# Feed-forward products by quarters with seven block products in place of eight

## The chip, the cores and the metric
The kernel runs on one core of a Trainium2 chip. Its engines are TensorE (PE, matmul), VectorE (DVE), ScalarE (ACT), GpSimd (POOL) and SyncE (SP, which issues the DMAs). The metric is the device time in microseconds: 1560.2 us is the median of three runs of the kernel before (1560.07 to 1561.64).

## The reference, cut to what matters
One layer of a hybrid encoder over 1024 tokens of 1024 channels: a norm and modulation, three token-mixing branches, a gated merge, an output projection with a residual, and a feed-forward of 4096 features with a squared ReLU.
```python
y = merged @ w_out
x = x + gate_m[:, None] * rmsnorm(y, g_mix_post)
h2 = rmsnorm(x, g_ff_pre) * (1.0 + scale_f[:, None]) + shift_f[:, None]
y2 = jnp.square(jax.nn.relu(h2 @ w_ff1)) @ w_ff2
return x + gate_f[:, None] * rmsnorm(y2, g_ff_post)
```
All is float32. The matrices of the two feed-forward products are 1024x1024 by 1024x4096, and 1024x4096 by 4096x1024.

## The kernel before
Every large product is made of two-part operands: a float32 tile a is split in hi (rounded to the fp32r format by ACT, line 99) and lo = a - hi (DVE, line 100), and each product takes three matmuls of 128x128 by 128x512: hi*hi, hi*lo, lo*hi. DVE's subtraction reads two SBUF operands.

The output projection (`out_tile`, L719 to L721) goes over eight token tiles of 128. The weights w_out come as eight raw tiles `wor` (L690), two in the buffers "raw" and six in the buffers "B", and are split to `woh` and `wol`. Behind each token tile stands a chain: squares of y on ACT (L722), a root with a Heron step (L212 to L219), the scaling by DVE (L729), the residual (L731), the store to x_d (L732), the second norm (L733, L735). `h2T_pair(tp, ...)` transposes two finished token tiles on PE (L744) and splits the result for the feed-forward (L752 to L755). The last pair's call stands inside the feed-forward: `ff1(0, ..., 0)`, then `h2T_pair(3, ...)`, then three more `ff1`.

The feed-forward goes over chunks of two feature tiles (the last of four). Per feature tile f, `ff1` makes u = relu(h2 @ w1)^2 for two halves of 512 tokens with 24 matmuls each (gemm_T, L327 to L329); ACT takes the ReLU from PSUM (L774), DVE squares (L775), and u is split. Then the chunk's u is multiplied with its two rows of w_ff2 for eight token tiles and two halves of the features (L820 to L822), and DVE adds the sum into `yacc` in SBUF (L827; one operand in PSUM). u never leaves SBUF. Per product of the feed-forward that is 8*32*2*3 = 1536 matmuls. POOL does nothing here until the end, where it multiplies by the gate row (L831). The last chunk's token tiles carry the final norm and the stores.

The instructions of each engine run in the order in which a scheduler puts them at build time. A tile whose tag has `bufs` buffers waits for the last reader of the tile that held its buffer before; one pool `big` holds all tiles for the whole program.

Of the kernel before, what the change touches and what calls it, by code (L numbers as in the profile page):

```python
# [51 lines left out]
def kernel(  # L52
# [389 lines left out]
    def att_scores(hd, cq, QS, KH, KL, nck):  # L442
        # softmax rows of queries 256 cq .. 256 cq + 255
# [43 lines left out]
    def att_values(hd, cq, Pt, att):  # L487
# [34 lines left out]
    def pool_unit(m):  # L522
# [4 lines left out]
        # trailing sums over 2, 4, 8, 16 tokens by doubling  # L527
# [103 lines left out]
    def mod_rows():  # L631
# [3 lines left out]
        # rows of gate * post-norm gain  # L635
# [36 lines left out]
        # the branches one after another for the last tile, which frees their operands earlier  # L672
# [28 lines left out]
    h2T = [None] * KT  # L701

    def out_tile(t):
        # x + gate * norm(merged @ w_out) for 128 tokens; the normalised result stays in xt
        tk = slice(t * P, (t + 1) * P)
        xt = sb("raw" if (t // 2) % 2 == 0 else "G", name="x2")
        nc.sync.dma_start(xt, x[t])
        mh = sb("whi", F32R, (P, KT, P), name="mh")
        ml = sb("wlo", F32R, (P, KT, P), name="ml")
# [4 lines left out]
        yt = sb("G", name="yt")  # L714
# [192 lines left out]
```

## Time and profile before
| | us |
|---|---|
| median of three runs | 1560.2 |
| span of the profiled execution | 1558.6 |
| PE busy | 1531.4 (98%) |
| DVE busy | 844.7 (54%) |
| ACT busy | 480.4 (31%) |
| POOL busy | 154.0 (10%) |

The profiled execution's span begins with its first instruction and ends with its last; the runs' times lie 1.5 us and more above it. A matmul's own duration is pipelined, so that the price of one in a row is the distance of two starts. "PE clock" in the rows is the granted clock as a share of the full one. The rows on which the prediction rests stand in a section of their own below.

### The profile page before, as it was taken

To read this page: it belongs to the slowest core of one execution; us is meant where nothing else is said; L and a number is where in the kernel's file an instruction comes from. 1 tells how busy PE (TensorE), PEld (TensorE's weight loads), DVE (VectorE), ACT (ScalarE), POOL (GpSimd) and SP (SyncE) were. 2 spreads that over 40 slices of the span, in tenths; PEclk is the share of its full clock that TensorE was granted. 3 is DMA by queue.
4 is the path that set the end of the run, shared out by engine and by line. 5 is a ranking of instruction groups with operands and counts; after the bars stand their busy time and mean duration, and the time that the engine had idled before them with its cause. 6 is when DMAs were issued, how large, how long until landed. Compare 5 with 4: busy or idle time off the path is not lost.

```text
span 1558.6 us, 18251 instructions
## 1 busy us (share of the span) xinstructions
PE 1531.4 (98%) x7115; PEld 1248.2 (80%) x7115; DVE 844.7 (54%) x1746; ACT 480.4 (31%) x876; POOL 154.0 (10%) x203
## 2 busy tenths in 40 slices
PE   6999999999999999999999999999999999999997
PEld 4897777777788888888888888888888888888886
DVE  7643578786685443222677344444444554444447
ACT  4612344445631111111555522221111222221132
POOL 6301323233300000000000000000000000000013
PEclk9999999999999999999999999999999999999999
DMA  7511101202344433111424111111111111111124
GB/s 255 195 41 55 41 28 55 82 28 77 126 162 146 152 123 94 46 49 55 149 81 148 56 55 54 54 41 41 41 44 52 54 55 54 54 41 48 46 82 162
DMA packets 37376, 125.63 MB, mean 81 GB/s; under 512 B 4825, under 2 KB 5929, under 8 KB 37290
## 3 DMA queue, kind: packets, MB, share of 16 engines
q1 hardware_dynamic: 37290, 124.47, 24.4%
q8 instruction: 56, 0.92, 0.3%
q14 instruction: 30, 0.25, 0.0%
HBM read 112.35 MB, written 12.10 MB: 80 GB/s over the span
## 4 chain that ended last, share of the span: by engine, by line
PE 93%; DVE 3%; ACT 2%; DMA 1%; issue 0%; SPq 0%; DVEq 0%; ACTq 0%
PE ps_mm L327 16%; PE ps_mm L329 16%; PE ps_mm L328 16%; PE ps_s L822 5%; PE ps_s L820 5%; PE ps_s L821 5%; PE ps_av L510 3%; PE ps_s L468 2%; PE ps_av L820 2%; PE ps_av L822 2%; PE ps_av L821 2%; PE ps_s L467 1%; PE ps_s L329 1%; PE ps_s L327 1%; PE ps_s L328 1%; PE ps_pt L504 1%
## 5 line engine op out<-in xcount | busy, mean ns | idle before, releaser
L327 PE MATMUL ps_mm<-hT,whi 128*128 128x512 f32 x592 | 235.0, 397 | 0.0
L329 PE MATMUL ps_mm<-hT,wlo 128*128 128x512 f32 x592 | 233.6, 395 | 0.0
L328 PE MATMUL ps_mm<-hT,whi 128*128 128x512 f32 x592 | 233.2, 394 | 0.0
L329 PE MATMUL ps_mm<-h2h,wlo 128*128 128x512 f32 x512 | 199.4, 389 | 0.0
L327 PE MATMUL ps_mm<-h2h,whi 128*128 128x512 f32 x512 | 199.4, 389 | 0.0
L328 PE MATMUL ps_mm<-h2l,whi 128*128 128x512 f32 x512 | 199.4, 389 | 0.0
L100 DVE TENSOR_TENSOR wlo<-wr,whi 128x1024 fp32r<-128x1024 f32 x60 | 73.5, 1224 | 179.6 <-ACT whi L99 179.4
L774 ACT ACTIVATE fr<-ps_mm 128x512 f32<-128x512 f32 x64 | 38.2, 597 | 419.9 <-PE ps_mm L329 419.9
L827 DVE TENSOR_TENSOR yacc<-yacc,ps_s 128x512 f32<-128x512 f32 (+1 forms) x155 | 105.4, 684 | 69.0 <-PE ps_s L822 68.7
L775 DVE TENSOR_TENSOR fr<-fr 128x512 f32<-128x512 f32 x64 | 44.3, 692 | 174.7 <-ACT fr L774 174.7
L821 PE MATMUL ps_s<-w2l,uh 128*128 128x512 f32 (+1 forms) x356 | 137.6, 387 | 0.0
L820 PE MATMUL ps_s<-w2h,uh 128*128 128x512 f32 (+1 forms) x356 | 137.6, 387 | 0.0
L822 PE MATMUL ps_s<-w2h,ul 128*128 128x512 f32 (+1 forms) x356 | 137.6, 387 | 0.0
L327 PEld LDWEIGHTS ps_mm<-hT,whi 128*128 128x128 f32 x592 | 111.2, 188 | 25.8 <-issue 3.8
L329 PEld LDWEIGHTS ps_mm<-hT,wlo 128*128 128x128 f32 x592 | 111.2, 188 | 24.1 <-issue 2.6
L328 PEld LDWEIGHTS ps_mm<-hT,whi 128*128 128x128 f32 x592 | 111.2, 188 | 23.9 <-issue 2.4
L831 POOL TENSOR_TENSOR yl<-yacc,gfb 128x512 f32<-128x512 f32 (+1 forms) x16 | 20.1, 1273 | 1070.2 <-DVE yacc L827 1066.9
L99 ACT ACTIVATE whi<-wr 128x1024 fp32r<-128x1024 f32 x60 | 63.7, 1061 | 172.2 <-PE ps_mm L328 88.5
L328 PEld LDWEIGHTS ps_mm<-h2l,whi 128*128 128x128 f32 x512 | 96.1, 188 | 19.9
L327 PEld LDWEIGHTS ps_mm<-h2h,whi 128*128 128x128 f32 x512 | 96.2, 188 | 19.9
L329 PEld LDWEIGHTS ps_mm<-h2h,wlo 128*128 128x128 f32 x512 | 96.1, 188 | 19.9
L821 PEld LDWEIGHTS ps_s<-w2l,uh 128*128 128x128 f32 x356 | 66.9, 188 | 13.6
(297 smaller groups left out, 2705.7 us busy)
## 6 DMA issues: line engine op xcount, KB each, us to landing
wa<-in_w_ada_dram SPq DMA_DIRECT2D x48, 512.0 KB, 5.3
wr<-in_w_in_dram SPq DMA_DIRECT2D x40, 512.0 KB, 3.6
wr<-in_w_ff_dram SPq DMA_DIRECT2D x32, 512.0 KB, 3.6
w2r<-in_w_ff_dram SPq DMA_DIRECT2D x32, 512.0 KB, 3.5
x<-in_x_dram SPq DMA_DIRECT2D x16, 512.0 KB, 3.7
nck<-nck_d SPq DMA_DIRECT2D x8, 512.0 KB, 3.7
wr<-in_w_branch_dram SPq DMA_DIRECT2D x8, 512.0 KB, 3.6
wor<-in_w_out_dram SPq DMA_DIRECT2D x8, 512.0 KB, 5.9
```

The lines of the kernel that those rows point to most:

```text
L99: A.activation(hi, src, AF.Copy)
L100: V.tensor_tensor(out=lo, in0=src, in1=f32(hi), op=ALU.subtract)
L327: T.matmul(p, a, r0, start=(i == 0), stop=False)
L328: T.matmul(p, a, r1, start=False, stop=False)
L329: T.matmul(p, b, r0, start=False, stop=(i == n - 1))
L510: last_pe[0] = T.matmul(av[:, :256], st, PT[:, pp, offs[jj]:offs[jj] + 256], start=(j == 0 and pp == 0), stop=(j == nj - 1 and pp == 1))
L774: A.activation(r, p, AF.Relu)
L775: V.tensor_tensor(out=r, in0=r, in1=r, op=ALU.mult)
L820: T.matmul(p, us[i][0][:, tk], w2[i][0][:, ns], start=(i == 0), stop=False)
L821: T.matmul(p, us[i][0][:, tk], w2[i][1][:, ns], start=False, stop=False)
L822: T.matmul(p, us[i][1][:, tk], w2[i][0][:, ns], start=False, stop=(i == n_f - 1))
L827: V.tensor_tensor(out=ya, in0=ya, in1=p, op=ALU.add)
```

## The change
Both feed-forward products are cut in 2x2 quarters, and each takes seven block products in place of eight, with sums of blocks on both sides (the variant of Strassen's scheme with the fewest sums).

- **First product.** With h2 in quarters B11, B12, B21, B22 (channels by tokens) and w_ff1 in pairs of tiles j and 16+j, each of the 16 steps j makes seven products of 12 matmuls: `first_two` two (banks X and Y), `last_five` five. 16*7*12 = 1344 matmuls. The sums on the weights' side are four POOL additions of 128x512 for each j (`prep_s`); the sums T1 to T4 on h2's side are made once, after `first_two` of j = 0 to 3 (EARLY), by 4*4 DVE and 4*4 POOL additions of 128x512, each sum split by ACT and DVE. u is squared by one DVE instruction (L854), and its quarters are written to the DRAM buffer u_d, four stores of 256 KB for each j.
- **Second product.** u is read back in quarters uA, uB, uC, uD, 32 loads of 512 KB (quarters 0, 1 and 3 stay in SBUF, 8 buffers each; uC has 2), and w_ff2, laid out by quarters, is read in 512 KB blocks. Seven rounds of eight steps of 24 matmuls: 7*8*24 = 1344. Every step has a split of u and one of w (two ACT, two DVE instructions of 128x1024); the sums of blocks are 48 POOL additions of 128x1024 and 16 on DVE (lines 999 and 1013). uh, ul, wh, wl and the raw tiles `w2r` have two buffers each. The rounds are called here, in their order: X (into p1), Y, Z, X2, X3, Z2, X5.
- **Order.** `h2T_pair(3, ...)` now stands before the first matmul of the feed-forward. The raw tiles of w_out share four buffers with the tiles of x. The pools are opened and closed by stage, and a tile of a later stage waits for those tiles of an earlier one whose place it takes.
- **End.** The final norm runs over the token tiles after the last product; the half that comes last is scaled on DVE for the lower four tiles.

The core of the diff:
```diff
+    wpool = open_pool("wpool", side="right")
+    h2pool = open_pool("h2pool")
+    opool = open_pool("opool")
...
     for k in range(KT):
-        raw = sb("raw" if k < 2 else "B", name="wor")
+        raw = tile_of(opool, "x2", 4, name="wor")
         nc.sync.dma_start(raw, w_out[k])
...
+    B11, B21, B22 = ([tile_of(h2pool, "h2", 12, HT, F32R, name=n) for _ in range(4)] for n in ("b11", "b21", "b22"))
+    B12 = [tile_of(h2pool, "b12", 4, (P, HALF)) for _ in range(4)]
...
+                b = B11[k] if k < 4 else (B22 if tp >= 2 else B21)[k - 4]
                 h = small.tile([P, 256], F32, tag="t256", name="h2t", bufs=2)
-                A.activation(h, p[:, kk * 256:(kk + 1) * 256], AF.Identity,
-                             bias=modc[:, 24 + k:25 + k], scale=af[:, k:k + 1])
-                V.tensor_copy(hi, h)
-                V.tensor_tensor(out=lo, in0=h, in1=f32(hi), op=ALU.subtract)
+                A.activation(h, src, AF.Identity, bias=modc[:, 24 + k:25 + k], scale=af[:, k:k + 1])
...
+    h2T_pair(3, pairs[3])
...
+    def prep_a(j):
+        r = load_half(j)
+        o = tile_of(fpool, "op", 4, (P, 2, D), F32R)
+        fsplit(o[:, 0, :], o[:, 1, :], r)
+        return r, o
+    def prep_s(j, r1):
+        r2 = load_half(NJ + j)
+        K1, K2 = slice(0, HALF), slice(HALF, D)
+        s21, s34 = (tile_of(mpool, "M", 8, name=n) for n in ("s21", "s34"))
+        G.tensor_tensor(out=s21[:, K2], in0=r2[:, K1], in1=r2[:, K2], op=ALU.add)
+        G.tensor_tensor(out=s21[:, K1], in0=s21[:, K2], in1=r1[:, K1], op=ALU.subtract)
+        o21 = tile_of(fpool, "op", 4, (P, 2, D), F32R)
+        fsplit(o21[:, 0, :], o21[:, 1, :], s21)
+        G.tensor_tensor(out=s34[:, K1], in0=r1[:, K1], in1=r2[:, K1], op=ALU.subtract)
+        G.tensor_tensor(out=s34[:, K2], in0=r1[:, K2], in1=s21[:, K1], op=ALU.subtract)
+        o34 = tile_of(fpool, "op", 4, (P, 2, D), F32R)
+        fsplit(o34[:, 0, :], o34[:, 1, :], s34)
+        o4 = tile_of(fpool, "oc", 1, HT, F32R)
+        fsplit(o4[:, 0, :], o4[:, 1, :], r2[:, K2])
+        return o21, o34, o4
+    def product(p, o, c0, bs, start):
+        for k in range(4):
+            ks = slice(c0 + k * P, c0 + (k + 1) * P)
+            a, b = o[:, 0, ks], o[:, 1, ks]
+            r0, r1 = bs[k][:, 0, :], bs[k][:, 1, :]
+            T.matmul(p, a, r0, start=(start and k == 0), stop=False, skip_group_check=True)
...
+    def relu2(q, j, c):
+        r = tile_of(fpool, "ur", 3, (P, HALF))
+        V.scalar_tensor_tensor(out=r, in0=c, scalar=0.0, in1=c, op0=ALU.max, op1=ALU.mult)
+        nc.sync.dma_start(u_d[q, j // 2, :, j % 2, :], r)
...
+    def first_two(j):
+        r1, o = prep_a(j)
+        X = fbank("X", 5)
+        product(X, o, 0, B11, True)
+        s1 = snap(X)
+        Y = fbank("Y", 1)
+        product(Y, o, HALF, B21, True)
+        relu2(0, j, plus(Y, s1))
+        return X, r1
+    def last_five(j, X, r1):
+        o21, o34, o4 = prep_s(j, r1)
+        product(X, o21, 0, T2, False)
+        u2 = snap(X)
+        Z = fbank("Z", 2)
+        product(Z, o21, HALF, T1, True)
+        p5 = snap(Z)
+        product(X, o34, 0, T3, False)
+        relu2(3, j, plus(X, p5))
+        product(Z, o34, HALF, B22, False)
+        relu2(2, j, plus(Z, u2))
+        product(X, o4, 0, T4, False)
+        c = tile_of(fpool, "sn", 3, (P, HALF))
+        A.activation(c, X, AF.Relu)
+        relu2(1, j, c)
+    begun = [first_two(j) for j in range(EARLY)]
+    T1, T2, T3, T4 = ([tile_of(tpool, "t", 16, HT, F32R, name=n) for _ in range(4)] for n in ("t1", "t2", "t3", "t4"))
...
+    for k in range(4):
...
+        tsum(V, ta, B12[k], h11, ALU.subtract)
+        tsum(V, ta, ta, l11, ALU.subtract)
+        fsplit(T1[k][:, 0, :], T1[k][:, 1, :], ta)
+        tsum(V, ta, h22, ta, ALU.subtract)
+        tsum(V, ta, ta, l22, ALU.add)
+        fsplit(T2[k][:, 0, :], T2[k][:, 1, :], ta)
+        tsum(G, tb, ta, h11, ALU.subtract)
+        tsum(G, tb, tb, l11, ALU.subtract)
+        fsplit(T3[k][:, 0, :], T3[k][:, 1, :], tb)
+        tc_ = tile_of(fpool, "ur", 3, (P, HALF), name="tt")
+        tsum(G, tc_, h21, ta, ALU.subtract)
+        tsum(G, tc_, tc_, l21, ALU.add)
+        fsplit(T4[k][:, 0, :], T4[k][:, 1, :], tc_)
...
+            last_five(j, *first_two(j))
...
+    def step(bank, kk, uop, wop, ts=range(4), first=False, last=False):
+        for k in range(2):
+            for t in ts:
+                tk = slice(t * P, (t + 1) * P)
+                a, b = uop[0][:, k, tk], uop[1][:, k, tk]
+                r0, r1 = wop[0][:, k, :], wop[1][:, k, :]
+                T.matmul(bank[t], a, r0, start=(first and k == 0), stop=False, skip_group_check=True)
...
+    def parts(u, w):
+        uh, ul = g2("uh", 2, F32R), g2("ul", 2, F32R)
+        fsplit(uh, ul, u)
+        wh, wl = g2("wh", 2, F32R), g2("wl", 2, F32R)
+        fsplit(wh, wl, w)
+        return (uh, ul), (wh, wl)
...
+    uA = [load_u(0, kk, "uA", NK) for kk in range(NK)]
+    X = banks("X")
+    for kk in range(NK):
+        step(X, kk, *parts(uA[kk], load_b(0, kk)), first=kk == 0, last=kk == NK - 1)
+    p1 = copies(X)
+    uB = []
+    Y = banks("Y")
+    for kk in range(NK):
+        uB.append(load_u(1, kk, "uB", NK))
+        step(Y, kk, *parts(uB[kk], load_b(2, kk)), first=kk == 0, last=kk == NK - 1)
+    c11 = sums(Y, p1)
+    uD, tt = [], []
+    Z = banks("Y")
+    for kk in range(NK):
+        s1 = load_u(2, kk, "uC", 2)
+        uD.append(load_u(3, kk, "uD", NK))
+        G.tensor_tensor(out=s1, in0=s1, in1=uD[kk], op=ALU.add)
+        t1 = load_b(1, kk, "tt", NK)
+        b11 = load_b(0, kk)
+        V.tensor_tensor(out=t1, in0=t1, in1=b11, op=ALU.subtract)
+        tt.append(t1)
+        step(Z, kk, *parts(s1, t1), first=kk == 0, last=kk == NK - 1)
+        G.tensor_tensor(out=uA[kk], in0=s1, in1=uA[kk], op=ALU.subtract)
+    p5 = copies(Z)
+    for kk in range(NK):
+        b22 = load_b(3, kk)
+        G.tensor_tensor(out=tt[kk], in0=b22, in1=tt[kk], op=ALU.subtract)
+        step(X, kk, *parts(uA[kk], tt[kk]), last=kk == NK - 1)
+    u2 = copies(X)
+    for kk in range(NK):
+        b11 = load_b(0, kk)
+        V.tensor_tensor(out=b11, in0=tt[kk], in1=b11, op=ALU.subtract)
+        s3 = g2("uC", 2, name="u")
+        G.tensor_tensor(out=s3, in0=uD[kk], in1=uA[kk], op=ALU.subtract)
+        step(X, kk, *parts(s3, b11), last=kk == NK - 1)
+    c22 = sums(X, p5)
+    for kk in range(NK):
+        b22 = load_b(3, kk)
+        G.tensor_tensor(out=uB[kk], in0=uB[kk], in1=uA[kk], op=ALU.subtract)
+        step(Z, kk, *parts(uB[kk], b22), last=kk == NK - 1)
+    c12 = sums(Z, u2)
+    ops = []
+    for kk in range(NK):
+        b21 = load_b(2, kk)
+        G.tensor_tensor(out=b21, in0=b21, in1=tt[kk], op=ALU.subtract)
+        ops.append(parts(uD[kk], b21))
+        if kk < NK - 2:
+            step(X, kk, *ops[kk])
...
+            E = V if t >= 4 and n == 0 else G
...
-    def ff1(f, wts, u, hf):
-        cs = slice(hf * HALF, (hf + 1) * HALF)
-        p = gemm_T(wts, h2T, K8, hf, "mm")
-        r = sb("G", name="fr", shape=(P, HALF))
-        A.activation(r, p, AF.Relu)
-        V.tensor_tensor(out=r, in0=r, in1=r, op=ALU.mult)
-        split(u[0][:, cs], u[1][:, cs], r)
...
-            ff1(0, w1[0], us[0], 0)
-            h2T_pair(3, pairs[3])
-            ff1(1, w1[1], us[1], 0)
...
-            for n, (a, b) in enumerate(((0, 512), (512, 768), (768, 1024)) if tail else ((0, 512), (512, 1024))):
...
-                    V.tensor_tensor(out=ya, in0=ya, in1=p, op=ALU.add)
...
+        "w_ff2": a["w_ff2"][0].reshape(2, 8, 2, P, 2, HALF).transpose(0, 4, 1, 3, 2, 5).reshape(4, 8, P, 2, HALF),
```

PE at the end of the output projection. Before: `ff1` of feature tile 0 (ps_mm_7343) is issued, then the transposes of the last pair (x_964 is its first token tile, read by L744) stand between it and the matmuls of feature tile 1.
```order
L328 MATMUL ps_mm_7343<-h2l_6723,whi_7329 128x512
L329 MATMUL ps_mm_7343<-h2h_6722,wlo_7330 128x512
L327 MATMUL ps_mm_7343<-h2h_6728,whi_7329 128x512
L328 MATMUL ps_mm_7343<-h2l_6729,whi_7329 128x512
L329 MATMUL ps_mm_7343<-h2h_6728,wlo_7330 128x512
L744 MATMUL ps_pt_7373<-ident,x_964_7077 128x128
L744 MATMUL ps_pu_7386<-ident,x_964_7077 128x128
L327 MATMUL ps_mm_7425<-h2h_6671,whi_7335 128x512
L328 MATMUL ps_mm_7425<-h2l_6672,whi_7335 128x512
L329 MATMUL ps_mm_7425<-h2h_6671,wlo_7336 128x512
```
Now the same place in the changed kernel, with L776 for the transposes (x_974 is the pair's second token tile) and X for the first block product, which reads the split weights op and the quarter B11 (b_904):
```order
L776 MATMUL ps_pt_7343<-ident,x_964_7095 128x128
L776 MATMUL ps_pt_7343<-ident,x_974_7232 128x128
L776 MATMUL ps_pu_7356<-ident,x_964_7095 128x128
L776 MATMUL ps_pu_7356<-ident,x_974_7232 128x128
L776 MATMUL ps_pu_7356<-ident,x_964_7095 128x128
L776 MATMUL ps_pu_7356<-ident,x_974_7232 128x128
L847 MATMUL X_7386<-b_904_6393,op_7383 128x512
L848 MATMUL X_7386<-b_904_6393,op_7383 128x512
L849 MATMUL X_7386<-b_904_6393,op_7383 128x512
L847 MATMUL X_7386<-b_905_6394,op_7383 128x512
```
All transposes of the last pair have moved ahead of the first feed-forward matmul.

ACT in the feed-forward. Before, a pattern of three repeats from feature tile to feature tile (fr is u before the split):
```order
L774 ACTIVATE fr_8524<-ps_mm_8499 128x512
L99 ACTIVATE uh_8497<-fr_8524 128x512
L99 ACTIVATE w2h_8561<-w2r_8559 128x1024
L774 ACTIVATE fr_8554<-ps_mm_8529 128x512
L99 ACTIVATE uh_8497<-fr_8554 128x512
L99 ACTIVATE whi_8769<-wr_8767 128x1024
L774 ACTIVATE fr_8598<-ps_mm_8573 128x512
```
Now, around the sums T1 to T4 (sn_7510 is the copy of X in step j = 3, op_7722 and op_7727 the split weight sums of j = 1, t_... the splits of T1 to T4, sn_7650 the first copy of `last_five`; rows for k = 1 to 3 of the sixteen splits are the same as those of k = 0):
```order
L812 ACTIVATE op_7722<-s_1050_7718 128x1024
L859 ACTIVATE sn_7510<-X_7497 128x512
L812 ACTIVATE op_7727<-s_1051_7719 128x1024
L812 ACTIVATE t_1008_7529<-tt_7545 128x512
L812 ACTIVATE t_1012_7533<-tt_7545 128x512
L812 ACTIVATE t_1016_7537<-tt_7546 128x512
L812 ACTIVATE t_1020_7541<-tt_7559 128x512
L812 ACTIVATE t_1019_7540<-tt_7603 128x512
L812 ACTIVATE t_1023_7544<-tt_7616 128x512
L859 ACTIVATE sn_7650<-X_7386 128x512
L859 ACTIVATE sn_7665<-Z_7652 128x512
```
The splits of T1 to T4 stand behind the split of a weight sum for j = 1 and ahead of the first copy of `last_five`.

POOL in the feed-forward. Before, it has only the products with the gate row at the end:
```order
L831 TENSOR_TENSOR yl_11549<-yacc_7527,gfb_7323 128x512 x2
L831 TENSOR_TENSOR yl_11598<-yacc_7544,gfb_7323 128x512 x2
L831 TENSOR_TENSOR yl_11647<-yacc_7561,gfb_7323 128x512 x2
L831 TENSOR_TENSOR yl_11696<-yacc_7578,gfb_7323 128x512 x2
L831 TENSOR_TENSOR yl_11745<-yacc_7595,gfb_7323 128x512 x2
```
Now, from the third sum s1 of the round Z on (u_10282: L996 makes s1, L1002 the X operand of the next round, L1021 an operand of Z2, L1007 the weight sums of X2; 20 rows from the first of these to s1 of the last step, u_10497):
```order
L1021 TENSOR_TENSOR u_9972<-u_9972,u_9600 128x1024
L996 TENSOR_TENSOR u_10325<-u_10325,u_10327 128x1024
L1002 TENSOR_TENSOR u_9602<-u_10325,u_9602 128x1024
L1021 TENSOR_TENSOR u_10008<-u_10008,u_9602 128x1024
L996 TENSOR_TENSOR u_10368<-u_10368,u_10370 128x1024
L1002 TENSOR_TENSOR u_9604<-u_10368,u_9604 128x1024
L1021 TENSOR_TENSOR u_10044<-u_10044,u_9604 128x1024
L996 TENSOR_TENSOR u_10411<-u_10411,u_10413 128x1024
L1002 TENSOR_TENSOR u_9606<-u_10411,u_9606 128x1024
L1021 TENSOR_TENSOR u_10080<-u_10080,u_9606 128x1024
L1007 TENSOR_TENSOR w2r_10201<-w2r_10548,w2r_10201 128x1024
L1007 TENSOR_TENSOR w2r_10244<-w2r_10583,w2r_10244 128x1024
```
Three additions of 128x1024 stand on POOL for each step of Z from the third on. Behind s1 of Z's last step stand six more up to the seventh weight sum of X2 (L1007 of w2r_10459), and DVE's queue has, ahead of the splits of X2's first step, the first subtraction of X3 (L1013, w2r_10836), whose load takes a raw buffer that this seventh weight sum reads.

## Rows read from the trace of the kernel before
**Rows 1.** Page: busy time of the engines (1), and the chain by engine (4).
```profile
PE 1531.4 (98%) x7115; PEld 1248.2 (80%) x7115; DVE 844.7 (54%) x1746; ACT 480.4 (31%) x876; POOL 154.0 (10%) x203
PE 93%; DVE 3%; ACT 2%; DMA 1%; issue 0%; SPq 0%; DVEq 0%; ACTq 0%
```
**Rows 2.** Windows: start:end, length, busy (count) by engine, PE clock, DMA share, GB/s.
```profile
900.00:1000.00 100.00, 99.97 (x442) 82.48 (x441) 47.60 (x62) 22.59 (x31) 0.00 (x0) 1.00 0.16 48
...
1554.00:1556.00 2.00, 0.00 (x0) 0.00 (x0) 1.57 (x3) 0.00 (x0) 0.00 (x0) 0.56 0.06 24
```
**Rows 3.** Timeline at the output projection's start: start, length, engine, line, out<-in.
```profile
725.59 11.16 SPq L690 DMA_DIRECT2D wor<-in_w_out_dram  x2
...
750.53 1.06 ACT L99 ACTIVATE woh<-wor 128x1024 fp32r<-128x1024 f32 x1 [3.58 <-DMA wor<-in_w_out_dram]
751.81 1.06 ACT L99 ACTIVATE woh<-wor 128x1024 fp32r<-128x1024 f32 x1 [0.22 <-DMA wor<-in_w_out_dram]
...
755.64 0.39 PE L329 MATMUL ps_s<-brh,wlo 128*128 128x512 f32 x1
755.86 0.39 PE L719 MATMUL ps_mm<-woh,mh 128*128 128x512 f32 x1
```
**Rows 4.** Timeline and chain around the last pair of token tiles.
```profile
849.24 0.39 PE L327 MATMUL ps_mm<-h2h,whi 128*128 128x512 f32 x1
...
849.18 0.24 PE ps_s L721
...
853.97 4.42 DMA x_d<-x
...
858.42 0.77 DVE x L735
...
859.23 0.56 PE ps_pt L744 x3
...
862.54 0.66 PE ps_pu L744 x4
863.20 0.23 PE ps_mm L327
```
**Rows 5.** Groups by line and form: count, busy us, mean ns, idle before.
```profile
L100 DVE TENSOR_TENSOR ul<-fr,uh 128x512 fp32r<-128x512 f32 x64 | 44.4, 693 | 35.3 <-ACT uh L99 34.9
L100 DVE TENSOR_TENSOR w2l<-w2r,w2h 128x1024 fp32r<-128x1024 f32 x32 | 39.1, 1225 | 7.7 <-ACT w2h L99 7.7
...
L831 POOL TENSOR_TENSOR yl<-yacc,gfb 128x512 f32<-128x512 f32 x15 | 19.1, 1293 | 1070.2 <-DVE yacc L827 1066.9 <-issue 3.2
...
L107 POOL TENSOR_SCALAR whi<-wr 128x1024 fp32r<-128x1024 f32 x17 | 18.7, 1101 | 136.3 <-PE ps_mm L328 97.4 <-PE ps_s L328 26.4 <-issue 8.2
...
L99 ACT ACTIVATE w2h<-w2r 128x1024 fp32r<-128x1024 f32 x32 | 33.3, 1044 | 0.0
```
**Rows 6.** Timeline of POOL and DVE, where both run.
```profile
29.02 2.38 POOL L114 TENSOR_TENSOR wlo<-wr,whi 128x1024 fp32r<-128x1024 f32 x1 [3.72 <-ACT whi L113]
...
29.49 2.45 DVE L260 TENSOR_TENSOR hT<-h,hT 128x512 fp32r<-128x512 f32 x1 [1.17 <-ACT hT L259]
...
40.37 2.38 POOL L114 TENSOR_TENSOR wlo<-wr,whi 128x1024 fp32r<-128x1024 f32 x1 [1.91 <-ACT whi L113]
...
40.84 2.45 DVE L260 TENSOR_TENSOR hT<-h,hT 128x512 fp32r<-128x512 f32 x1 [2.37 <-ACT hT L259]
```
**Rows 7.** Timeline of PE near the program's start.
```profile
22.39 0.63 PE L327 MATMUL ps_av<-hT,whi 128*128 128x512 f32 x1
22.82 0.63 PE L328 MATMUL ps_av<-hT,whi 128*128 128x512 f32 x1
```
**Rows 8.** DMA issues: KB each, median us from issue to landing.
```profile
w2r<-in_w_ff_dram SPq DMA_DIRECT2D x32, 512.0 KB, 3.5
...
out_dram<-yl SPq DMA_DIRECT2D x16, 256.0 KB, 2.0
```
**Rows 9.** Timeline of PE, its last matmul.
```profile
1549.24 0.28 PE L822 MATMUL ps_s<-w2h,ul 128*128 128x256 f32 x1
```

More of the change, by code (lines that the diff above doesn't have):

```diff
@@ L762, with fbank, fsplit @@
         pairs.append((x0, out_tile(2 * tp + 1)))
-    yacc = [None] * NT
-    gfb = sb("G", name="gfb")
+    h2T_pair(3, pairs[3])
+    close_pool("opool")
+    close_pool("wpool")
+    close_pool("psum")
+    fpool = open_pool("fpool")
+    tpool = open_pool("tpool", side="right")
+    fps = open_pool("fps", space=bass.MemoryType.PSUM)
+    def fbank(tag, bufs):
+        return tile_of(fps, tag, bufs, (P, HALF))
+    def fsplit(hi, lo, src):
+        A.activation(hi, src, AF.Copy)
+        V.tensor_tensor(out=lo, in0=src, in1=f32(hi), op=ALU.subtract)
@@ new lines, in snap, with plus @@
+    def snap(p):
+        s_ = tile_of(fpool, "sn", 3, (P, HALF))
+        A.activation(s_, p, AF.Copy)
+        return s_
+    def plus(p, s_):
+        V.tensor_tensor(out=s_, in0=p, in1=s_, op=ALU.add)
+        return s_
+    def first_two(j):
[22 more added lines that the diff above has]
+        relu2(1, j, c)
@@ new lines, with g2, load_u @@
+    for j in range(NJ):
+        if j < EARLY:
+            last_five(j, *begun[j])
+        else:
+            last_five(j, *first_two(j))
+    for n in ("fpool", "h2pool", "mpool", "tpool", "fps"):
+        close_pool(n)
+    gpool = open_pool("gpool")
+    gps = open_pool("gps", space=bass.MemoryType.PSUM)
+    NK = NJ // 2
+    UT = (P, 2, HALF)
+    def g2(tag, bufs, dtype=F32, shape=UT, name=None):
+        return tile_of(gpool, tag, bufs, shape, dtype, name)
+    def load_u(q, kk, tag, bufs):
+        r = g2(tag, bufs, name="u")
+        nc.sync.dma_start(r, u_d[q, kk])
+        return r
@@ new lines, in load_b @@
+    def load_b(q, kk, tag="wr", bufs=2):
+        r = g2(tag, bufs, name="w2r")
+        nc.sync.dma_start(r, w_ff2[q, kk])
+        return r
+    def step(bank, kk, uop, wop, ts=range(4), first=False, last=False):
[5 more added lines that the diff above has]
+                T.matmul(bank[t], a, r0, start=(first and k == 0), stop=False, skip_group_check=True)
+                T.matmul(bank[t], a, r1, start=False, stop=False, skip_group_check=True)
+                T.matmul(bank[t], b, r0, start=False, stop=(last and k == 1), skip_group_check=True)
@@ new lines, in parts, with banks, copies @@
+    def parts(u, w):
[4 more added lines that the diff above has]
+        return (uh, ul), (wh, wl)
+    def banks(tag):
+        return [tile_of(gps, tag, 4, (P, HALF)) for _ in range(4)]
+    def copies(bank):
+        r = []
+        for t in range(4):
+            s_ = g2("sn", 12, shape=(P, HALF))
+            A.activation(s_, bank[t], AF.Copy)
+            r.append(s_)
+        return r
@@ new lines, in sums @@
+    def sums(bank, ss):
+        for t in range(4):
+            V.tensor_tensor(out=ss[t], in0=bank[t], in1=ss[t], op=ALU.add)
+        return ss
+    uA = [load_u(0, kk, "uA", NK) for kk in range(NK)]
[8 more added lines that the diff above has]
+        step(Y, kk, *parts(uB[kk], load_b(2, kk)), first=kk == 0, last=kk == NK - 1)
@@ new lines @@
+    c22 = sums(X, p5)
[11 more added lines that the diff above has]
+            step(X, kk, *ops[kk])
+    for t in range(4):
+        for kk in (NK - 2, NK - 1):
+            step(X, kk, *ops[kk], ts=(t,), last=kk == NK - 1)
@@ new lines @@
+    for t in range(NT):
+        half = [(c11, c12), (c22, X)][t // 4]
+        order = ((0, half[0][t % 4]), (1, half[1][t % 4])) if t < 4 else ((1, half[0][t % 4]), (0, half[1][t % 4]))
+        xt, yl = g2("uA", NK, shape=(P, D), name="x2r"), g2("uB", NK, shape=(P, D), name="yl")
+        nc.sync.dma_start(xt, x2_d[t])
+        for n, y in order:
+            ns = slice(n * HALF, (n + 1) * HALF)
+            sq = g2("uC", 2, shape=(P, HALF), name="sq")
+            A.activation(sq, y, AF.Square, accum_out=ssf[:, t, n:n + 1])
+            E = V if t >= 4 and n == 0 else G
+            E.tensor_tensor(out=yl[:, ns], in0=y, in1=gfb[:, ns], op=ALU.mult)
+        V.tensor_tensor(out=ssf[:, t, 0:1], in0=ssf[:, t, 0:1], in1=ssf[:, t, 1:2], op=ALU.add)
+        rstd(ssf[:, t, 0:1], rsf[:, t:t + 1])
+        for n, _ in order:
+            ns = slice(n * HALF, (n + 1) * HALF)
+            V.scalar_tensor_tensor(out=yl[:, ns], in0=yl[:, ns], scalar=rsf[:, t:t + 1], in1=xt[:, ns],
+                                   op0=ALU.mult, op1=ALU.add)
+            nc.sync.dma_start(out[0, t * P:(t + 1) * P, ns], yl[:, ns])
```

126 lines of the change are left out of this document (52 added, 74 removed).

## The prediction
> **What bounds the kernel now.** I read the page's busy times and its chain by engine first: PE is busy for 98% of the span and makes 93% of the chain [rows 1]. The reader is to see there that nothing else bounds it: DVE has 54%, POOL 10%. Then the windows: between 900 and 1000 us, deep in the feed-forward, PE has 442 matmuls in 100 us at the full clock, and POOL none [rows 2]. That is 100/442 = 0.226 us per matmul, at 2.4 GHz. The feed-forward runs from 849.24 us [rows 4] to the last matmul at 1549.24 [rows 9]. Last come the places where the change cuts into this: the starts of the stages, and the rows in which POOL and DVE run side by side.
>
> **What it removes.** 2*(1536 - 1344) = 384 matmuls, 384*0.226 = 86.9 us of PE. On a PE at 98% that is the whole gain, unless PE waits. In the kernel before it hardly does at a change of stage. So what counts is every wait that is new. I go through the program in order; "stall" is PE time beyond its matmuls.
>
> **Start of the output projection.** Before, two raw tiles of w_out are asked for from 725.59 on, and the first split starts at 750.53 [rows 3], so PE goes on from 755.64 to 755.86 without a gap. Now the raw tiles have four buffers, taken from the stage before, whose last readers are the last branch product. A load takes 3.5 us [rows 8], the ACT split 1.04 [rows 5], so the first product can start at about 758.5, and the later tiles follow 1.28 us apart [rows 3], behind which the first token tile lasts a little longer: **+3** (0 to 5).
>
> **Last pair of token tiles.** Before, the last product of the projection is followed by `ff1` at once, and the pair's chain runs under it: x_d store at 853.97, 4.42 us, DVE x at 858.42, transposes at 859.23, the last at 862.54 to 863.20 [rows 4]. Now the transposes stand before the first feed-forward matmul on PE, although that one reads only B11, which is long there. PE idles from 849.2 to the transposes, and the first weight split stands behind the evacuations on ACT: it begins at about 865, **+15.8** (12 to 17).
>
> **First product.** 1344*0.226 = 304.0 us. In the steady steps 84 matmuls give 19.0 us per j, in which DVE has about 9.3, POOL 4*1.29 = 5.2 [rows 5], ACT about 6: hidden, 0 (0 to 8).
>
> **Sums T1 to T4.** The four `first_two` fill 96*0.226 = 21.7 us, but the splits of the sums stand on ACT behind the split of a weight sum that takes a buffer which Y of step 3 reads to its end, so the chain begins only when they are over. Per k it has 8 DVE subtractions at 0.69 and 4 POOL additions at 1.29 [rows 5], 5.5 + 5.2 = 10.7, and DVE's lo of T3 and T4 waits for POOL's sums of the same k. Whether the two engines overlap is the question of the whole change, so here are the rows: a POOL subtraction from 29.02 to 31.40 lies across a DVE subtraction of 128x512 that starts at 29.49 and takes 2.45 us; the same at 40.37 and 40.84 [rows 6]. DVE's form of that size takes 0.69 [rows 5]. It ended 0.54 us after POOL's, which is its own work. So I take it that DVE, reading two SBUF operands, waits until POOL's two-operand instruction is over, and the other way round. The Trainium skill ("SBUF — State Buffer", section "Who interferes with whom") says that a DVE instruction with two SBUF inputs contends with a GpSimd instruction that reads SBUF, over an exclusive lock; by that rule the sum is the one I take, and the trace agrees (2.45 against 0.69 us). With the exclusion a k takes about 11.0 us, and T4 of k = 3 is ready some 48.8 us after the last Y; without it, 8.7 us and 38.9. PE has, of `last_five` of step 0, the 48 matmuls before the product with T4 to do, 10.9 us. Stall **+38** (28 without exclusion).
>
> **From the first to the second product.** SP issues the loads of uA behind the last store of u, and w2r of the first step as the ninth load: from the last matmul, 2.1 us of ReLU and square, 3.5 of load, 8*1.28 of queue [rows 3, 8], ACT 1.04 and DVE 1.22 [rows 5] make 18.1. **+18** (12 to 24).
>
> **Second product.** 1344*0.226 = 304.0 us, 5.4 per step. The steps of rounds X and Y need two DVE splits, 2.4 us, and no POOL: no stall. In **Z** POOL has, from the third s1 to that of the last step, 20 additions, one after the other since uC has two buffers, and its load waits for the split of s1 two steps before: 20*2.38 = 47.6 us [rows 6]. DVE has to put 20 instructions of 1.22 us (24.4) with two SBUF inputs between them. With the exclusion the two add up: 72 us, and a last split and step of about 11, so Z ends some 83 us after Y, against 43.6 for its matmuls: **+40** (+12 without: 47.6 + 2.3 + 5.4 = 55.3). Then **X2**: its first splits stand on DVE behind the first subtraction of X3, whose load takes the buffer that POOL's seventh weight sum reads, six additions (14.3 us) behind that last s1; with load, subtraction and two splits PE starts some 13 us after the end of Z: **+13** (10 to 15, with or without exclusion). **X3** has per step three DVE instructions and one of POOL, 3.67 + 2.38 = 6.05 against 5.4: **+5** (0 without). **X5**, with the weight sum on POOL beside the final norm's first instructions: **+4** (1 without).
>
> **End.** The last matmul to the end took 1558.6 - 1549.24 = 9.4; the new tail has one half token tile less to wait for: 8.
>
> **Clock.** After PE had stopped, the granted clock was 0.56 in the window 1554 to 1556 [rows 2], and near the start, with PE in short bursts, two matmuls stood 0.43 us apart (22.39, 22.82) [rows 7], which is 1.2 GHz. Each matmul after a long gap would cost 0.2 us more until the clock is back. The four gaps may cost 0 to 4 us each; I take 1 each: **+4** (0 to 15).
>
> **Sum**, on the profiled execution: 849.2 + 3 + 15.8 + 304 + 38 + 18 + 304 + 40 + 13 + 5 + 4 + 8 + 4 = 1606.0. The median of the runs lies 1.6 above the span, so **1607.6**: 3% slower. New stalls of some 140 us stand against 86.9 saved.
>
> **Rivals.**
> - *POOL and DVE overlap freely.* Then T costs 28, Z 12, X3 0 and X5 1: 849.2 + 3 + 15.8 + 304 + 28 + 18 + 304 + 12 + 13 + 0 + 1 + 8 + 4 + 1.6 = 1561.6, about no change, and with the low ends of the stage changes 1545. For it: the DVE form with an operand in PSUM, which most of this kernel's DVE work has, is no witness against it. Against it: both pairs of rows 6.
> - *Faster: POOL's two-operand sums cost what its one-operand form costs*, 1.1 us for 128x1024 [rows 5]. Its place is Z and the X2 start: 20*1.1 + 24.4 = 46 us, so Z stays within 3 us of its matmuls and the six additions ahead of X2 shrink to 6.6 and are over before Z ends; T loses some 10. Time: 849.2 + 3 + 15.8 + 304 + 28 + 18 + 304 + 3 + 0 + 0 + 1 + 8 + 4 + 1.6 = 1539.6. It decides as soon as a POOL sum takes less than about 1.6 us. Against it: 1.29 for half the size, and 2.38 [rows 5, 6].
> - *Slower still: PE's clock stays at its low level where matmuls come in bursts*, as they do in Z: with some 200 matmuls behind the four gaps at 0.43 instead of 0.226 the sum gains 40: about 1645. For it: rows 7. Against it: in Z PE waits for DVE anyway, so that a slower PE costs nothing there.
> - *The saving doesn't appear*: that a block product is really seven for eight can be counted, 1344 for 1536, so I give this nothing.
>
> **How the numbers follow.** The forecast case has 0.62; free overlap 0.18, of which I count half as faster (its stage changes at their low ends), a quarter as no change; the cheap POOL 0.08; the low clock 0.12. A difference under about 0.2% (3 us) can't be told from no change. Faster: 0.09 + 0.08 = 0.17; the same: 0.045, taken as 0.05; slower: 0.78. The forecast's own range is 1585 to 1635: 10 us on T, 15 on Z and X2, 6 on the first load, the clock. The range to hold 8 in 10 takes in free overlap down to 1553 and reaches into the low clock up to 1640.
>
> **What would show it.** In the new profile: PE's idle time before its first X product released by DVE x and ACT; one gap of 30 to 40 us behind the fourth `first_two`, with DVE lines 813 and 896 and POOL line 896 alternating; about 18 us before the first matmul of the second product, released by the load of w2r; in Z, POOL's additions 2.4 us each with hardly a pause, and DVE's splits well above 1.22 us; DVE's first L1013 waiting for a DMA. If DVE's mean in Z is 1.22 and POOL's rows overlap it, the exclusion is wrong, and with it 45 us. If POOL's rows are near 1.1, the second rival holds. If PE has no gap at the sums T1 to T4, my reading of ACT's order was wrong.

## The result: 4.5% slower, and the profile after

The changed kernel takes 1631.15 us (median of four runs, 1630.13 to 1633.4) against 1560.92: ratio 1.0452, 95% interval 1.0437 to 1.0467. The forecast was 1607.6, slower; the direction and the range (1585 to 1635) held, and the sum was 23.5 us short.

The page: busy times and chain, to set beside [rows 1].
```profile
span 1631.6 us, 18102 instructions
PE 1508.1 (92%) x6719; PEld 1199.1 (73%) x6719; DVE 949.1 (58%) x1663; ACT 551.2 (34%) x934; POOL 422.1 (26%) x327
PE 83%; DVE 7%; POOL 4%; ACT 2%; issue 2%; DMA 2%; SPq 0%; DVEq 0%; ACTq 0%; POOLq 0%
```
PE is busy for 23 us less, not 87, and idle for 123 us of the span, where it was idle for 27. POOL's busy time has grown by 268 us.

The gaps of PE in order (timeline of PE; in brackets the idle time and what ended it):
```profile
773.62 1.22 PE L751 MATMUL ps_mm<-woh,mh 128*128 128x512 f32 x2 [5.13 <-ACT woh L114]
...
879.82 0.90 PE L776 MATMUL ps_pt<-ident,x 128*128 128x128 f32 x3 [7.86 <-DVE x L767]
...
885.00 0.80 PE L847 MATMUL X<-b,op 128*128 128x512 f32 x1 [1.15 <-ACT op L812]
...
909.04 0.39 PE L849 MATMUL Y<-b,op 128*128 128x512 f32 x1
916.13 0.79 PE L847 MATMUL Z<-t,op 128*128 128x512 f32 x1 [6.71 <-ACT t L812]
...
955.48 0.80 PE L847 MATMUL X<-t,op 128*128 128x512 f32 x1 [3.40 <-ACT sn L859]
...
1254.08 1.22 PE L950 MATMUL X<-wh,uh 128*128 128x512 f32 x2 [17.82 <-ACT wh L812]
...
1436.59 0.79 PE L951 MATMUL X<-wl,uh 128*128 128x512 f32 x1 [8.61 <-DVE wl L813]
...
1588.67 0.79 PE L951 MATMUL X<-wl,uh 128*128 128x512 f32 x1 [6.40 <-DVE wl L813]
```
Each stage change of the forecast is there: the output projection's start, the last pair, the sums T1 to T4 (909 to 955), the first load of the second product, the start of X2, and X5.

The third round. POOL and DVE beside each other in the changed kernel:
```profile
1356.70 3.38 POOL L996 TENSOR_TENSOR u<-u,u 128x1024 f32<-128x1024 f32 x1
1360.16 3.21 POOL L1002 TENSOR_TENSOR u<-u,u 128x1024 f32<-128x1024 f32 x1
1363.45 3.20 POOL L1021 TENSOR_TENSOR u<-u,u 128x1024 f32<-128x1024 f32 x1
...
1354.40 6.76 DVE L999 TENSOR_TENSOR w2r<-w2r,w2r 128x1024 f32<-128x1024 f32 x2
1361.09 3.37 DVE L813 TENSOR_TENSOR ul<-u,uh 128x1024 fp32r<-128x1024 f32 x1
1364.38 3.35 DVE L813 TENSOR_TENSOR wl<-w2r,wh 128x1024 fp32r<-128x1024 f32 x1
```
One of each takes turns: both read 3.2 to 3.4 us, where DVE alone needs 1.22 [rows 5] and POOL 2.38 [rows 6]. The windows of Y (1302.78 to 1346) and of Z (columns as in [rows 2]):
```profile
1302.78:1346.00 43.22, 43.05 (x190) 35.34 (x189) 23.48 (x19) 16.58 (x18) 2.64 (x2) 1.00 0.55 187
1346.00:1427.59 81.59, 57.86 (x197) 44.49 (x196) 61.95 (x24) 17.82 (x19) 76.48 (x26) 0.81 0.38 118
```
Z takes 81.6 us for the matmuls that Y does in 43.2. POOL is busy for 76.5 of them.

What no stage change explains shows first in code that the change doesn't touch. Windows of 100 us in the projections from hT (untouched) and in the first feed-forward product (time, length, PE busy with its count of matmuls, PE clock, DMA share, GB/s), of the kernel before:
```profile
600.00:700.00 100.00, 100.00 (x444) 1.00 0.17 48
1000.00:1100.00 100.00, 100.00 (x443) 1.00 0.18 58
```
and of the changed one:
```profile
600.00:700.00 100.00, 100.00 (x433) 1.00 0.16 50
1000.00:1100.00 100.00, 100.00 (x434) 1.00 0.32 109
```
PE is busy all the time at the full clock and starts 2.0 to 2.5% fewer matmuls. The starts show which. Between the first two rows lie 144 starts of matmuls with hT as one operand, 0.234 us each; between the second and the third lie 47 starts of the branches, 0.227 us each.
```profile
723.69 0.40 PE L344 MATMUL ps_mm<-hT,whi 128*128 128x512 f32 x1
...
757.42 0.39 PE L344 MATMUL ps_s<-brh,whi 128*128 128x512 f32 x1
...
768.10 0.39 PE L346 MATMUL ps_s<-brh,wlo 128*128 128x512 f32 x1
```

### The profile page after: what moved, and what is told of

Same layout as the page of the kernel before. It is cut to its first block, busy times and chain, and to the rows that moved or that the text cites. A ratio compares the mean times of both kernels' runs of the same rounds, so it can differ in the third digit from the quotient of the medians.

```text
span 1631.6 us, 18102 instructions
## 1 busy us (share of the span) xinstructions
PE 1508.1 (92%) x6719; PEld 1199.1 (73%) x6719; DVE 949.1 (58%) x1663; ACT 551.2 (34%) x934; POOL 422.1 (26%) x327
## 4 chain that ended last, share of the span: by engine, by line
PE 83%; DVE 7%; POOL 4%; ACT 2%; issue 2%; DMA 2%; SPq 0%; DVEq 0%; ACTq 0%; POOLq 0%
PE ps_mm L344 9%; PE ps_mm L346 9%; PE ps_mm L345 9%; PE X L847 4%; PE X L849 4%; PE X L848 4%; PE X L951 3%; PE X L952 3%; PE X L950 3%; PE ps_av L527 2%; PE ps_s L485 2%; PE Z L847 2%; PE Z L848 2%; PE Z L849 2%; POOL tt L896 1%
## 5 line engine op out<-in xcount | busy, mean ns | idle before, releaser
L813 DVE TENSOR_TENSOR ul<-u,uh 128x1024 fp32r<-128x1024 f32 x56 | 85.6, 1529 | 114.5 <-ACT uh L812 114.5
L812 ACT ACTIVATE uh<-u 128x1024 fp32r<-128x1024 f32 x56 | 59.3, 1059 | 210.8 <-PE X L951 104.5
L951 PE MATMUL X<-wl,uh 128*128 128x512 f32 x256 | 103.4, 404 | 17.5 <-DVE wl L813 17.5
L950 PE MATMUL X<-wh,uh 128*128 128x512 f32 x256 | 102.0, 400 | 18.0 <-ACT wh L812 18.0
L813 DVE TENSOR_TENSOR wl<-w2r,wh 128x1024 fp32r<-128x1024 f32 x56 | 98.7, 1762 | 8.6 <-ACT wh L812 8.2
L951 PE MATMUL Y<-wl,uh 128*128 128x512 f32 x192 | 80.9, 421 | 23.4 <-DVE wl L813 23.4
L952 PE MATMUL X<-wh,ul 128*128 128x512 f32 x256 | 102.1, 399 | 0.0
L950 PE MATMUL Y<-wh,uh 128*128 128x512 f32 x192 | 78.9, 411 | 0.5 <-ACT wh L812 0.5
L952 PE MATMUL Y<-wh,ul 128*128 128x512 f32 x192 | 79.2, 413 | 0.0
L500 POOL TENSOR_SCALAR prob<-prob,sm 128x128 f32<-128x128 f32 (+3 forms) x64 | 51.8, 809 | 100.8 <-DVE sm L499 97.6
```

The costliest lines, as they stand in the source:

```text
L500: G.tensor_scalar(pr_[:, :L], pr_[:, :L], sm, 0.0, op0=ALU.mult, op1=ALU.add)
L812: A.activation(hi, src, AF.Copy)
L813: V.tensor_tensor(out=lo, in0=src, in1=f32(hi), op=ALU.subtract)
L950: T.matmul(bank[t], a, r0, start=(first and k == 0), stop=False, skip_group_check=True)
L951: T.matmul(bank[t], a, r1, start=False, stop=False, skip_group_check=True)
L952: T.matmul(bank[t], b, r0, start=False, stop=(last and k == 1), skip_group_check=True)
```

## The experiments

### The operands' place in SBUF
The slow matmuls read hT, woh/wol or T1 to T4, the tiles of the right-hand pools. The addresses stand in the compiled program, not in a view of the profile. There hT starts at byte 163808 of each partition and whi at 147264: 16544 apart, 160 modulo 512. In the kernel before, hT starts at 105312 and whi at 212832, a multiple of 512 apart, and of its 5848 matmuls with 512 columns all but 62 have their operands a multiple of 256 apart.

**Right-hand tiles 32 bytes lower.**
```diff
+    pad = ctx.enter_context(tc.tile_pool(name="pad", bufs=1, side="right"))
+    pad_t = pad.tile([P, 8], F32, name="pad_t")
```


> The changed kernel with one 32-byte tile put at the end of SBUF, so that all tiles of the right-hand pools (hT, woh/wol, T1 to T4) start 32 bytes lower; nothing else differs. In the changed kernel the matmuls that read these as the moving operand start 0.2345 us apart, all others 0.227; the right-hand tiles start at 32 modulo 64 bytes, the stationary operands there at 0. Theory (the two operands of a matmul must start at the same offset modulo 64 bytes for the full rate): now both are at 0, so these about 3100 matmuls go back to 0.227, about 22 us less: 1609. Rival (the upper end of SBUF, or the right-hand pools themselves, are slow): 1631, no change.


Measured: 1628.72 us, 2.4 less. The theory of 64 bytes fell: both operands now start at 0 modulo 64, the distance is 128 modulo 512, and matmuls from hT are still 0.233 us apart.

**The kernel before, weights 32 bytes higher.**
```diff
+        if tag == "whi" and "padw" not in BUFS:
+            G.memset(big.tile([P, 8], F32, tag="padw", name="padw", bufs=1), 0.0)
```


> The kernel before with one 32-byte tile ahead of the weight buffers whi and wlo, so that they (and mh, ml in the same buffers) start at 0 modulo 64 bytes while the moving operands stay at 32; nothing else differs. Theory (same offset modulo 64 needed): some 4000 matmuls, 1776 of the projections, 384 of the branches, 384 of the output projection and 1440 of the first feed-forward product, go from 0.227 to 0.2345 us: 30 us more, 1591; the second feed-forward product, whose operands are in other buffers, stays. Rival (only the place at the upper end of SBUF counts, or only the moving operand's own offset): 1560, no change.


Measured: 1583.64 us, 22.8 more (ratio 1.0148, 1.0133 to 1.0163). Only an offset has changed; the operands didn't move to the end of SBUF. The same window as above:
```profile
600.00:700.00 100.00, 100.00 (x432) 1.00 0.16 48
```
The rival, the place at the end, is out. Spread over some 4000 matmuls, 22.8 us are 0.006 us each.

**Right-hand tiles 160 bytes lower**, which makes the distance 16384 bytes.
```diff
+    pad_t = pad.tile([P, 40], F32, name="pad_t")
```


> The changed kernel with 160 bytes at the end of SBUF in place of the 32 of the first offset run, so that the right-hand tiles and the buffers of the other operand start at the same offset modulo 512 bytes. So far matmuls were fast (0.227 us apart) where the two operands' starts differ by a multiple of 512 bytes, and slow (0.233 to 0.235) where the difference is 32, 128 or 160 modulo 512. Theory (the difference must be 0 modulo some size above 128): the 3100 matmuls return to 0.227, 22 us less than the changed kernel: 1609. Rival (tiles near the end of SBUF are slow, and the 32 bytes of the first run brought a little by chance): about 1629.


Measured: 1612.89 us, 18.3 less than the changed kernel. Both windows are back:
```profile
600.00:700.00 100.00, 100.00 (x443) 1.00 0.16 48
1000.00:1100.00 100.00, 100.00 (x442) 1.00 0.31 106
```
No run was made for a distance of 256, but two kernels hold one: the weights of the first feed-forward tile lie elsewhere, 256 modulo 512 from h2, and the 32 bytes put ahead of the weight buffers don't move them. In the kernel before, their first 24 matmuls from 849.24 on [rows 4] are 0.227 us apart. In the kernel with those 32 bytes the first and last of these 24, and then of 24 with the moved weights (480 modulo 512), are
```profile
863.47 0.39 PE L330 MATMUL ps_mm<-h2h,whi 128*128 128x512 f32 x1
...
868.71 0.40 PE L332 MATMUL ps_mm<-h2h,wlo 128*128 128x512 f32 x1
...
909.94 0.39 PE L330 MATMUL ps_mm<-h2h,whi 128*128 128x512 f32 x1
...
915.30 0.40 PE L332 MATMUL ps_mm<-h2h,wlo 128*128 128x512 f32 x1
```
or 0.228 and 0.233 us for each of 23 starts. So the matmuls ran at the full rate where the two operands were a multiple of 256 bytes apart, and at no other distance that occurs here in number. One rival stays untested: the operands of these fast matmuls all start at 64 or 96 modulo 256, and each of the slow ones has one that starts at 128, 192 or 224, so a rule on each operand's own start would fit as well as one on the distance.

### POOL against DVE
**Sums of the second product on DVE.**
```diff
-        G.tensor_tensor(out=s1, in0=s1, in1=uD[kk], op=ALU.add)
+        V.tensor_tensor(out=s1, in0=s1, in1=uD[kk], op=ALU.add)
```
and the same in the five other lines with block sums on POOL.


> The changed kernel with the 48 sums of blocks of the second product on DVE instead of POOL; nothing else differs. Theory (POOL and DVE exclude each other, so that each pair costs about 3.3 us of both): DVE's splits fall back from 3.3 to 1.22 us in the third round, five DVE instructions a step are 6.1 us against 5.4 of PE, the round lasts about 52 us instead of 81, the wait of 9 us ahead of X2 shrinks below 4, and X5 loses 6 of its 9: about 1590. Rival (DMA of u and w_ff2 or the two-buffer tags set the round): the round stays near 80 us, 1625 to 1640.


Measured: 1572.60 us, 58.5 less, more than expected. Y and Z together, 384 matmuls, in the window
```profile
1299.37:1386.40 87.03, 87.03 (x385) 72.05 (x384) 66.53 (x60) 34.80 (x37) 0.00 (x0) 1.00 0.55 176
```
have no idle PE at all, though DVE does 48 instructions more: the mean of wl, the low part of the split weights, falls from 1762 to 1240 ns, first with the sums on POOL and then with them on DVE:
```profile
L813 DVE TENSOR_TENSOR wl<-w2r,wh 128x1024 fp32r<-128x1024 f32 x56 | 98.7, 1762 | 8.6 <-ACT wh L812 8.2
L813 DVE TENSOR_TENSOR wl<-w2r,wh 128x1024 fp32r<-128x1024 f32 x56 | 69.4, 1240 | 7.8 <-ACT wh L812 7.7
```
Z gives 38 us, X2 and X3 12, X5 7, X 3. It was expected that five DVE instructions per step (6.1 us) would hold PE. In a row they start 1.13 us apart (1284.49, 1285.62, 1286.76), and eight of the sums of the later rounds were done under X and Y.

**Memsets in place of the sums** (the sums are left out).
```diff
+    def no_sum(t):
+        for _ in range(2):
+            G.memset(t, 0.5)
-        G.tensor_tensor(out=s1, in0=s1, in1=uD[kk], op=ALU.add)
+        no_sum(s1)
```


> The changed kernel with each of POOL's 48 sums of the second product replaced by two POOL memsets of the same 128x1024 tile, which read nothing from SBUF (the sums are left out, so the output is another); DVE's work is the same. It parts POOL's own length from its exclusion with DVE. Theory (POOL's reads exclude DVE's second SBUF operand): with two memsets of about 1 us each POOL is as busy as a sum alone (2.2 to 2.4 us), but DVE's splits take 1.22 us beside it, POOL's memsets don't grow, and the third round falls from 81 us to 45 to 55; about 1590 in all. Rival (the two slow each other on any access to SBUF): DVE's splits stay near 3 us and the round near 80: about 1630.


Measured: 1572.99 us. POOL and DVE in that third round:
```profile
1345.28 1.97 POOL L980 MEMSET u<- 128x1024 f32 x2 [0.92 <-DMA u<-u_d]
1348.19 1.97 POOL L980 MEMSET w2r<- 128x1024 f32 x2 [0.94 <-DVE wl L813]
...
1345.78 1.22 DVE L813 TENSOR_TENSOR ul<-u,uh 128x1024 fp32r<-128x1024 f32 x1
1348.05 2.36 DVE L1003 TENSOR_TENSOR w2r<-w2r,w2r 128x1024 f32<-128x1024 f32 x2
```
They overlap and neither grows: 1.97 us for two memsets, 1.22 and 1.18 for DVE. POOL that only writes didn't hold DVE here. The Trainium skill ("SBUF — State Buffer", section "Who interferes with whom") says the same: a DVE instruction with two SBUF inputs contends with a GpSimd instruction that reads SBUF, not with one that only writes it. The run agrees, with 1.22 us against 3.35. Since two memsets are 0.4 us shorter than a sum, and depend on less, the run doesn't part the exclusion's price from POOL's own length to the microsecond.

### The stage changes
**Loads of uA in the steps.**
```diff
-    uA = [load_u(0, kk, "uA", NK) for kk in range(NK)]
+        uA.append(load_u(0, kk, "uA", NK))
```


> The changed kernel with the loads of uA issued step by step, each just ahead of its weight block, instead of eight in a row ahead of the first weight block; nothing else differs. Theory (the gap of 18.2 us ahead of the second product is the first weight block's place as ninth load in the queue): seven loads of 1.28 us leave the path, gap about 9, 9 us less: 1622. Rival (the gap is the round trip of u through DRAM itself, store and load, whatever the order): the gap stays at 17 to 18 us, 1631.


Measured: 1622.73 us, 8.4 less; the gap is half as long:
```profile
1243.99 1.22 PE L950 MATMUL X<-wh,uh 128*128 128x512 f32 x2 [8.89 <-ACT wh L812]
```

**Sums T1 to T4 one k behind each first_two.**
```diff
-    begun = [first_two(j) for j in range(EARLY)]
+        begun.append(first_two(k))
```


> The changed kernel with the sums T1 to T4 of k = 0 to 3 put behind first_two of j = k in the program, one k each, instead of all behind the fourth; nothing else differs. Theory (the stall of 36 us is the chain of these sums, which starts only when the four first_two are over because it shares buffers with them and stands behind them on ACT): the chain starts some 16 us earlier but shares DVE with the splits of the four steps, 11 to 13 us per k in place of 9.8: stall 20 to 26, 10 to 16 us less: 1618. Rival (the sums' own wait is for the last pair of token tiles or for PE): 1631, no change.


Measured: 1628.71 us, 2.4 less: a miss. The chain does start earlier (896 in place of 911), but takes 14 to 19 us for each of the first three k in place of 9.8, since DVE now takes turns with POOL's sums of weights too and has the steps' own splits between. Its end moves by 2 us.

### Versions put together
**The sums on DVE, the loads in the steps and the 160 bytes**, the three edits shown above, in one kernel.


> Three edits together: the 48 sums of the second product on DVE (58.5 us less alone), the loads of uA in step (8.4 less alone), the 160 bytes at the end of SBUF. Theory: they lie in different stages and add up: 1631 - 58.5 - 8.4 - 22 = 1542, below the kernel before (1560.8). Rival (with the right-hand offset no cure): 1564.


Measured: 1545.42 us (ratio 0.9898, 0.9883 to 0.9913). With the 18.3 us of the offset as measured, the sum of the three is 1545.9: they add up.

**And the sums T1 to T4 behind each first_two, all on DVE.**
```diff
-        tsum(G, tb, ta, h11, ALU.subtract)
+        tsum(V, tb, ta, h11, ALU.subtract)
```
and so for the three others.


> The same three edits, and the sums T1 to T4 put one k behind each first_two and all on DVE (12 instructions of 0.69 us per k, 8.3 us, in place of 9.8 with POOL). Theory: the chain starts at the first step and is 4*8.3 us plus four times 2.6 us of the steps' own DVE work, 44 us from the end of step 0, against 27 us of PE work: stall near 15 instead of 36: 1542 - 20 = 1522. Rival (the order of ACT or the buffers hold it back): 1535 to 1542.


Measured: 1536.01 us (0.9838, 0.9824 to 0.9853), 9.4 less than the one before, but less than expected. Two things changed at once, the order of the sums and their engine; the order alone, with POOL, gave 2.4, and DVE alone wasn't run, so that their shares stay open.

**Transposes of the last pair behind the second first_two.**
```diff
+            with tc.issue_after(last_of[0][0].ins), tc.issue_after(last_of[0][1].ins):
+                h2T_pair(3, pairs[3])
```


> The kernel with all earlier edits (1536.0 us), and the transposes of the last pair of token tiles queued behind the second first_two on PE (through the two Z banks; the normalised tiles in two of the free M buffers), T1 to T4 behind the fourth. Theory (PE waits 13 us for this pair's chain although its next products don't need it): the first product starts when its weight split is there, 5 to 8 us earlier, of which the chain of T sums, now later by its place in the program, takes some back: 1528 to 1533. Rival (the T sums are the longer chain from this pair to the next products, so that nothing is gained): 1536 or a little more.


Measured: 1541.37 us, 5 more: the rival. PE's first product starts only 1.8 us earlier (869.3, 871.1), and the T sums start later (900.2 in place of 881.5). The weight split, behind the pair's norm on ACT, then waits for its load, which SP issues only from 863.25 on, behind the pair's stores:
```profile
850.00 13.20 SPq L767 DMA_DIRECT2D x_d<-x  x2
863.25 2.96 SPq L820 DMA_DIRECT2D w1r<-in_w_ff_dram  x5
...
868.20 2.22 ACT L815 ACTIVATE op<-w1r 128x1024 fp32r<-128x1024 f32 x2 [3.85 <-DMA w1r<-in_w_ff_dram]
```

**Five first_two ahead.**
```diff
-EARLY = 4
+EARLY = 5
```


> The kernel of 1536.0 us (sums of the second product on DVE, loads in step, 160 bytes offset, T sums on DVE behind each first_two) with five first_two ahead of the last five products in place of four. Theory (the chain of T sums, some 50 us from the first step, is what PE waits for, and a fifth step adds 24 matmuls, 5.4 us, under it): 1531. Rival (the fifth step's own splits stand on DVE in the same chain, 2.6 us and two buffers, or its X bank, the last of five, holds back the step after it): 1534 to 1540.


Measured: 1532.18 us (0.9812, 0.9796 to 0.9829), as expected: 1.9% faster than the kernel before. The change is worth having once its sums leave POOL, its operands are aligned and its stage changes are reordered.

## Why the prediction was right or wrong

| step | forecast | measured |
|---|---|---|
| up to the last branch product | 0 | +12.5 (768.10, before 755.64) |
| start of the output projection | +3 | +5.3 |
| the projection itself | 0 | +4.6 |
| last pair of token tiles | +15.8 | +13.4 |
| sums T1 to T4 | +38 | +35.3 (909.27 to 955.48 less 48 matmuls) |
| rest of the first product, its start taken in | 0, and clock | +11.8 |
| first to second product | +18 | +18.0 |
| X | 0 | +5.3 |
| Z | +40 | +37.9 (with Y) |
| X2 and X3 | +13 and +5 | +12.3 |
| X5 | +4 | +9.6 |
| end | 8 | 8.1 |

- **Right, by its mechanism.** The exclusion of POOL and DVE set Z (2.38 + 1.22 = 3.60 expected for a pair, 3.2 to 3.4 measured: they overlap by a few tenths). The free-overlap rival fell with the rows of Z, the cheap-POOL rival with sums of 2.33 us and more. That the exclusion is about reads is shown by the memsets; that the sums on POOL cost 58 us here is shown by the sums on DVE, though the exclusion's share of it can't be parted fully from that of POOL's length.
- **Right, by its working.** The queue of loads: 18.0 against 18, and half of it went when the loads were reordered. T: 35.3 against 38, with 9.8 us per k in place of 11.0. The X2 start: 8.6 us of idle PE, released by DVE behind a first L1013 that waited 13.1 us for its load:
```profile
1432.46 1.80 DVE L1013 TENSOR_TENSOR w2r<-w2r,w2r 128x1024 f32<-128x1024 f32 x1 [13.12 <-DMA w2r<-in_w_ff_dram]
```
- **The step that failed**: "1344*0.226 = 304.0 us" for the first product, and the unsaid same price for all products that the change left as they were. 0.226 is the price at one placing of the tiles. The new pools moved hT, woh/wol and T1 to T4 to a distance of 160 modulo 512 bytes, and some 3100 matmuls took 0.234. Undoing the distance alone gave back 18.3 of the 23.5 us that the sum was short. Some 12 of these 18.3 us lay ahead of the change (768.10 against 755.64; 756.47 in the kernel of 1536.0 us, which has the 160 bytes), where the forecast started its sum at the row of before. Nothing in the diff says it; the tiles' addresses do. That the other terms, each up to about 6 us off, left only some 5 us together is luck.
- **Sizes off.** X5, POOL and DVE of the changed kernel:
```profile
1578.24 5.16 POOL L1028 TENSOR_TENSOR w2r<-w2r,w2r 128x1024 f32<-128x1024 f32 x2
...
1578.53 5.42 DVE L1058 SCALAR_TENSOR_TENSOR yl<-yl,rsf,x2r 128x512 f32<-128x512 f32 x2
```
  Two instructions of the final norm, 0.75 us each when alone, took 5.42 ahead of the splits: 6.4 us of idle PE, and 9.6 for the round in place of 4. X had two steps that waited for DVE beside POOL's first sums (1.39 and 0.93 us idle), which the forecast had put into Z. X2 and X3 together cost 12.3 in place of 18: PE has no idle time over 0.3 us in X3, so that the +5 of X3 didn't appear.
- **Clock.** Forecast +4 in a term of its own; it is inside the rows above. Outside T and Z some 46 matmuls behind the gaps start 0.40 to 0.45 us apart (the granted clock is 0.50, 1.2 GHz, from 1436 to 1442), 0.2 us more each, so it cost about 9. Z's window has 0.81, and there PE waited for DVE, so that a slow PE cost little if anything, as the slower rival's own counter-argument said; no run parts it.

## What to carry to other kernels
Two-operand sums on an idle POOL aren't free beside a DVE that reads two SBUF operands: here DVE alone did 48 more of them and the kernel was 58 us faster. After any change of pools, compare the starts of the matmuls that weren't touched with those of before, and where the two operands of each start, modulo 256 bytes. A saving of PE work by sums on other engines has to be paid at each change of stage: look at what stands ahead in every queue there.

## What the runs showed of the hardware that was not expected
A 128x128 by 128x512 fp32r matmul started every 0.227 us where its two operands in SBUF began a multiple of 256 bytes apart, and every 0.233 to 0.234 us where the distance was 32, 128 or 160 bytes off such a multiple: 444 against 432 to 434 in 100 us, with PE busy and at the full clock in both. Whether the distance counts or each operand's own start modulo 256 isn't shown. Thirty-two bytes ahead of the weight buffers alone made a kernel 1.5% slower.
